# Merge gates of a two-layer hybrid trunk: seven block products for each pair of feature tiles in place of eight

## The chip, the cores and the metric

One core of one Trainium2 chip runs the whole program. The metric is the device time of one execution in microseconds (us), as a median of several runs. The core has five engines that work from queues of their own: PE (TensorE, matmuls; its weight loads are shown apart as PEld), DVE (VectorE), ACT (ScalarE), POOL (GpSimd) and SP (SyncE, which here issues all DMAs). Each engine takes its instructions in the order in which they stand in its queue, and a semaphore holds one back until what it needs is there.

## The reference, cut to what matters

Two layers run over 640 tokens (128 of context, 512 of latents) and 1024 features. Each layer makes `h` from `x`, projects it for four mixers (A: RWKV recurrence, B: attention, C: gMLP, D: Fourier), and merges their outputs with gates that come from `h`:

```python
h = rms_norm(x, p['norm_g']) * (1.0 + scale) + shift
...
proj = jnp.einsum('nbtw,nwd->nbtd', jnp.stack([o_a, o_b, o_c, o_d]), p['w_branch'])
gates = jax.nn.sigmoid(h @ p['w_merge'] + p['b_merge']).reshape(B, T, N_BRANCH, D_MODEL)
merged = jnp.einsum('nbtd,btnd->btd', proj, gates)
x = x + gate * (merged @ p['w_out'])
```

`h @ w_merge` is a product of (640 x 1024) by (1024 x 4096) in each layer, four gates for each of the 1024 features. The change is about this product. The Fourier branch is the real part of a 2-D DFT over positions and the 128 channels of each of four groups.

## The kernel before, in words

Features stand on partitions and tokens on columns. A feature tile is 128 features by T = 640 tokens; the tokens are worked on in two halves of 320 columns (`HALVES`). All big products are made with split operands: an f32 matrix is stored as `hi` (rounded to fp32r) plus `lo` (the rest), and a product is three matmuls, hi·hi, hi·lo and lo·hi, summed in PSUM (lines 168, 169, 170 in `dense_half`). `split` (lines 144 and 145) makes the parts: ACT casts `hi`, then POOL, or DVE where the call says so, subtracts to get `lo`. Weights come from HBM as raw blocks of 128 x 512 (`wr`, 4 buffers) and are split into `wh` and `wl` (3 buffers each), so that the split of a block may run up to three blocks ahead of PE.

The order of the work is written as Python generators: a main generator and a side generator are stepped in turn (`mix`), the side at a rate given for the stage. A scheduler then moves instructions within each engine's queue by its own estimate of times, so that casts, loads and side work stand ahead of where they were written. The queues are then fixed.

The end of each layer is the merge. For each branch n, in the order 1, 2, 3, 0 (attention, gMLP, Fourier, recurrence), and each of 8 feature tiles m it makes a gate (`gate`: 8 blocks of 128 inputs x 3 matmuls x 2 halves = 48 matmuls of 320 columns, then a tanh on ACT, line 1140) and a branch product (`branch`: 4 x 3 x 2 = 24 matmuls, then on DVE line 1146, which multiplies by the gate, and line 1149, which adds to `mg`). Beside each of the four stages runs a side generator (`beside`): `gmlp` beside branch 1, `fourier` beside branch 2, `rec_out` (group norm and bonus of the recurrence's output) beside branch 3, and beside branch 0 the conditioning (`ada`) of the next layer; layer 0 also has two steps of `ada` after `rec_out`. The results of a side generator go to HBM (`odr`) and are read back by `load_o` for the next stage. After the last branch each tile of `mg` is split into `mh` and `ml` for the output product.

`rec_out` loads five rows (`rv`) for each of four channel groups, and for each group makes three sums over 64 channels with matmuls against a block of ones (`sums`, lines 1082 and 1083, into the small PSUM banks named m), with some 20 DVE operations on 128 x 640 around them (lines 1093 to 1116).

PSUM has 8 banks. In the recurrence and the merge 3 are for the big products (`dps`) and 5 for side work (m).

## Time and profile before

| | us |
|---|---|
| median of 3 runs (2328.18 to 2330.07) | 2329.81 |
| profiled execution | 2330.01 |
| its span, first to last instruction | 2328.1 |
| PE busy in the span | 2183.5 |
| DVE busy | 1449.2 |
| ACT busy | 1098.4 |
| POOL busy | 894.4 |

A busy time is the union of an engine's instructions. Matmuls are pipelined, so that one of 0.31 us starts 0.147 us after the one before it; a busy PE is therefore not always a PE at its peak, and the count of matmuls in a stretch times the distance between their starts says more. The merge of layer 0 lies at 714.7 to 1138 us and that of layer 1 at 1865 to 2258.6 us of the span. Rows of a stretch list its length, then for each engine the busy time and in brackets the number of instructions, the granted clock of PE as a share of its full speed, and what the DMA engines did.

### The profile page before, as it was taken

How to read it: one execution, taken by the hardware profiler on the slowest of the kernel's cores; microseconds unless marked ns; L12 is line 12 of the kernel's file. 1: busy time of each engine (PE TensorE's matmuls, PEld its weight loads, DVE VectorE, ACT ScalarE, POOL GpSimd, SP SyncE). 2: the span in 40 equal slices, each digit the busy share in tenths (PEclk: the TensorE clock that was granted, in tenths of full speed). 3: DMA queues.
4: the chain of work that ended last, by engine and by line, in shares of the span. 5: the costliest groups of instructions: out<-in, count | busy, mean ns of one | idle time of the engine just before them, and what ended most of it. 6: DMA issues, size and time to landing. Idle time of an engine off the chain costs nothing. (4 is left out here: it accounts for less than half of the span.)

```text
span 2328.1 us, 49632 instructions
## 1 busy us (share of the span) xinstructions
PE 2183.5 (94%) x19662; PEld 2013.7 (86%) x19662; DVE 1449.2 (62%) x2826; ACT 1098.4 (47%) x2387; POOL 894.4 (38%) x894
## 2 busy tenths in 40 slices
PE   6899998898999999899999999989999999998998
PEld 3788898787888999878998888978888899997997
DVE  4777757888884335822367787578889643367234
ACT  4566755444434334422355676544444343344332
POOL 2322224444433335523552212244444334355452
PEclk8999999999999999999999999999999999998999
DMA  7133336333215425565432323362332254264233
GB/s 262 51 108 95 93 98 194 101 100 100 85 56 177 143 80 179 155 219 203 151 98 87 105 81 99 115 197 86 99 88 70 62 178 152 76 187 147 91 102 106
DMA packets 208009, 283.73 MB, mean 122 GB/s; under 512 B 26912, under 2 KB 119712, under 8 KB 207776
## 3 DMA queue, kind: packets, MB, share of 16 engines
q1 hardware_dynamic: 207776, 280.55, 38.1%
q8 instruction: 155, 2.54, 0.5%
q14 instruction: 78, 0.64, 0.1%
HBM read 224.75 MB, written 55.74 MB: 120 GB/s over the span
## 5 line engine op out<-in xcount | busy, mean ns | idle before, releaser
L145 POOL TENSOR_TENSOR wl<-wr,wh 128x512 fp32r<-128x512 f32 x371 | 523.0, 1413 | 975.0 <-ACT wh L144 853.4
L168 PE MATMUL dps<-hhi,wh 128*128 128x320 f32 x2368 | 772.6, 326 | 10.8 <-DVE f L1146 4.2
L169 PE MATMUL dps<-hlo,wh 128*128 128x320 f32 x2368 | 744.7, 314 | 7.9 <-POOL hlo L302 4.5
L170 PE MATMUL dps<-hhi,wl 128*128 128x320 f32 x2368 | 742.2, 313 | 0.0
L168 PEld LDWEIGHTS dps<-hhi,wh 128*128 128x128 f32 x2368 | 452.7, 191 | 25.6 <-ACT hhi L300 4.8
L169 PEld LDWEIGHTS dps<-hlo,wh 128*128 128x128 f32 x2368 | 453.3, 191 | 14.6 <-POOL hlo L302 7.1
L170 PEld LDWEIGHTS dps<-hhi,wl 128*128 128x128 f32 x2368 | 452.1, 191 | 0.5
L144 ACT CAST wh<-wr 128x512 fp32r<-128x512 f32 x372 | 229.6, 620 | 311.0 <-PE dps L169 200.2
L168 PE MATMUL dps<-ohi,wh 128*128 128x320 f32 x512 | 161.6, 316 | 2.1 <-ACT wh L144 1.9
L170 PE MATMUL dps<-ohi,wl 128*128 128x320 f32 x512 | 158.7, 311 | 1.0 <-POOL wl L145 1.0
L822 DVE TENSOR_TENSOR XZ<-XZ,m 128x512 f16<-128x512 f16 x200 | 129.5, 677 | 47.4 <-PE m L819 47.3
L169 PE MATMUL dps<-olo,wh 128*128 128x320 f32 x512 | 159.0, 311 | 0.0
L1146 DVE SCALAR_TENSOR_TENSOR f<-f,dps 128x320 f32<-128x320 f32 x96 | 46.3, 486 | 169.3 <-PE dps L170 169.3
L769 POOL TENSOR_TENSOR GG<-GG,con 64x256 f32<-64x256 f32 x80 | 60.8, 760 | 163.8 <-DVE GG L764 160.6
L1140 ACT ACTIVATE f<-dps,der 128x320 f32<-128x320 f32 x128 | 67.2, 525 | 111.4 <-PE dps L170 104.1
L168 PEld LDWEIGHTS dps<-ohi,wh 128*128 128x128 f32 x512 | 97.0, 189 | 10.6 <-issue 5.9
L170 PEld LDWEIGHTS dps<-ohi,wl 128*128 128x128 f32 x512 | 96.6, 189 | 2.4 <-POOL wl L145 1.5
L169 PEld LDWEIGHTS dps<-olo,wh 128*128 128x128 f32 x512 | 96.9, 189 | 1.7 <-issue 1.7
L812 DVE TENSOR_TENSOR T<-m,con 128x256 f16<-128x256 f32 x200 | 80.7, 416 | 18.6 <-PE m L811 18.0
L774 ACT CAST A<-GG 64x256 f16<-64x256 f32 x80 | 32.3, 403 | 90.4 <-POOL GG L769 90.3
L615 DVE TENSOR_TENSOR pl<-m,ph 128x512 fp32r<-128x512 f32 (+1 forms) x96 | 59.1, 620 | 24.8 <-ACT ph L614 23.5
L818 PE MATMUL m<-T,XZ 128*128 128x64 f16 x800 | 66.0, 195 | 5.2 <-DVE T L812 5.2
(493 smaller groups left out, 4624.4 us busy)
## 6 DMA issues: line engine op xcount, KB each, us to landing
wr<-in_w_in SPq DMA_DIRECT2D x180, 256.0 KB, 2.9
wr<-in_w_merge SPq DMA_DIRECT2D x128, 256.0 KB, 2.7
ar<-in_w_ada SPq DMA_DIRECT2D x48, 512.0 KB, 6.3
wr<-in_w_branch SPq DMA_DIRECT2D x64, 256.0 KB, 2.8
zdr<-f SPq DMA_DIRECT2D x48, 320.0 KB, 3.4
rk<-spill SPq DMA_DIRECT2D x20, 768.0 KB, 5.9
thdr<-t SPq DMA_DIRECT2D x32, 320.0 KB, 3.2
odr<-t SPq DMA_DIRECT2D x32, 320.0 KB, 3.5
```

The source lines that it names most:

```text
L144: S_.copy(hi, src)
L145: (leng or G).tensor_sub(lo, src, hi.bitcast(F32))
L168: mm(ps, hi[:, c], ahi(k)[:, q], start=(k == 0), stop=False)
L169: mm(ps, hi[:, c], alo(k)[:, q], start=False, stop=False)
L170: mm(ps, lo[:, c], ahi(k)[:, q], start=False, stop=(k == K - 1))
L615: V.tensor_sub(pl[:, 0:w], tp[:, 0:w], ph[:, 0:w].bitcast(F32))
L769: G.tensor_sub(GK[HALF[j], j], GK[HALF[j], j], bc(i64[HALF[j]], 4))
L812: V.tensor_mul(T1.rearrange("p u (j k o i) -> p (u j) k o i", j=2, o=2, i=b)[:, :, :, 0, :], ps[:, 0:256].rearrange("p (x k i) -> p x k i" ...
L818: mm(ps[:, 64 * u:64 * u + 64], X1[:, u, :], cols(T1[:, u, :], 0), start=True, stop=True)
L822: V.tensor_add(new, new, ps.rearrange("p (x n i) -> p x n i", x=2, i=b))
L1140: yield from dense(A["w_merge"][l, m, n], 8, H, lambda q, ps: S_.activation(gt[:, q], ps, AF.Tanh, scale=0.5, bias=bias))
L1146: yield from dense(A["w_branch"][l, n, m], 4, (lambda k: o[k][0], lambda k: o[k][1]), lambda q, ps: V.scalar_tensor_tensor(to[:, q], gt[:, ...
```

## The change

The gates of two neighbouring feature tiles m and m+1 are one product of a 256 x 1024 weight matrix by the 1024 x 640 `h`. Cut in 2 x 2 blocks on every side (two tiles, two halves of the inputs, two halves of the tokens) it takes eight block products of 4 x 3 = 12 matmuls each. The changed kernel makes it with seven, by Strassen's algorithm in Winograd's form. For that:

- `sums_of_h` makes three combinations T1, T2, T4 of the four blocks of `h` once in each layer, and `last_sum_of_h` a fourth, T3, which is written over a block of `h` that is needed no more.
- for each pair, DVE makes four combinations of the raw weight blocks (`s1`, `a21`, `a11`, `a12` in place); these are then split and multiplied by `product`.
- the products are collected in three PSUM banks: `al` takes four of the seven products one after the other and is read in between, `ga` takes two and is read in between, `be` takes one. Copies on ACT and additions on DVE put the parts of the four results together in `g`.
- the `al` bank is a pool of its own ("a"), so that the side work has 4 small banks where it had 5.
- the first two pairs of the first stage (`PLAIN = 2`) are made as before, in eight products, so 14 of the 16 pairs of a layer use seven.

The side work is put in another order: branches go 1, 0, 2, 3; beside branch 1 stand `sums_of_h` and `rec_out`, beside branch 0 `gmlp` (in layer 0 with two steps of `ada` behind it), beside branch 2 `fourier`, beside branch 3 the `ada` of the next layer. The rates are new. The buffers of `rec_out` are cut: three of its five rows have one buffer in place of two. `load_o` has 8 buffers where it had 12, and its loads for a branch are all issued after the second product of the branch's first pair. The Fourier mixing runs for two groups at a time, with the transform of its first column made for each two groups (15 small matmuls more in each layer). `gmlp` writes its gate input back to HBM and loads it again. The split of `mg` reuses the buffers of `mg`.

```diff
-RATE_M = (0.3, 0.55, 0.8, 0.5)
+RATE_M = (0.75, 0.45, 0.6, 0.45)
+PLAIN = 2
+SRB = 4
...
         def rec_out(y):
...
-                    rv = gp.tile([128, 5, T], F32, tag="rv", name="rv")
+                    rv = []
                     for i, (src, row) in enumerate(((spill, c), (spill, 12 + c), (spill, 4 + c), (thdr, 4 + c), (thdr, 12 + c))):
-                        nc.sync.dma_start(rv[:, i, :].rearrange("p (c t) -> p c t", t=128), src[l][:, :, row, :].rearrange("c p t -> p c t"))
+                        rv.append(gp.tile([128, T], F32, tag=f"rv{i}", name=f"rv{i}", bufs=2 if i > 2 else 1))
+                        nc.sync.dma_start(rv[i].rearrange("p (c t) -> p c t", t=128), src[l][:, :, row, :].rearrange("c p t -> p c t"))
...
+        def hsum(kk, top, q):
+            ks = slice(4 * top + 2 * kk, 4 * top + 2 * kk + 2)
+            t = tmp().rearrange("p (k t) -> p k t", k=2)
+            V.tensor_add(t, h_hi[:, ks, q].bitcast(F32), h_lo[:, ks, q].bitcast(F32))
+            return t
+        def sums_of_h(tp, B):
+            for n in ("1", "2", "4"):
+                B["T" + n] = tuple(tp.tile([128, 4, 320], F32R, name=f"T{n}{x}") for x in "hl")
+            for kk in range(2):
...
+                t1 = hsum(kk, 0, Q0)
+                t = hsum(kk, 0, Q1)
+                V.tensor_sub(t1, t, t1)
+                put("T1", t1)
+                yield
+                t2 = hsum(kk, 1, Q1)
+                V.tensor_sub(t2, t2, t1)
+                put("T2", t2)
...
+        def last_sum_of_h(B):
+            for kk in range(2):
+                ks = slice(2 * kk, 2 * kk + 2)
+                a, b = hsum(kk, 1, Q1), hsum(kk, 0, Q1)
+                V.tensor_sub(a, a, b)
+                S_.copy(h_hi[:, ks, Q1], a)
+                V.tensor_sub(h_lo[:, ks, Q1], a, h_hi[:, ks, Q1].bitcast(F32))
...
+        def product(ps, raw, b, leng, first=True):
+            hi, lo = (wp.tile([128, 512], F32R, tag="w" + x, name="w" + x, bufs=3) for x in "hl")
+            split(hi, lo, raw, leng)
+            for k in range(4):
+                c = slice(128 * k, 128 * k + 128)
+                mm(ps, hi[:, c], b[0][:, k, :], start=first and k == 0, stop=False, skip_group_check=True)
+                mm(ps, hi[:, c], b[1][:, k, :], start=False, stop=False, skip_group_check=True)
+                mm(ps, lo[:, c], b[0][:, k, :], start=False, stop=(k == 3), skip_group_check=True)
...
+                a11, a12 = raw_load(src[0], 512), raw_load(src[1], 512)
+                a21, a22, s1 = (m1.tile([128, 512], F32, tag="sr", name="sr", bufs=SRB) for _ in range(3))
...
+                yield from product(al, a11, B["11"], G)
+                S_.copy(g[0][:, Q0], al)
+                V.tensor_add(s1, a21, a22)
+                V.tensor_sub(a21, a11, a21)
+                V.tensor_sub(a11, s1, a11)
+                yield from product(be, a12, B["21"], V)
+                V.tensor_add(g[0][:, Q0], g[0][:, Q0], be)
+                tanh(0, Q0)
+                V.tensor_sub(a12, a12, a11)
+                start(n)
+                yield from product(ga, s1, B["T1"], G)
+                S_.copy(g[1][:, Q1], ga)
+                yield from product(al, a11, B["T2"], V, False)
+                S_.copy(g[0][:, Q1], al)
+                yield from product(ga, a12, B["22"], G, False)
+                V.tensor_add(g[0][:, Q1], g[0][:, Q1], ga)
+                tanh(0, Q1)
+                yield from product(al, a21, B["T3"], V, False)
+                V.tensor_add(g[1][:, Q1], g[1][:, Q1], al)
+                tanh(1, Q1)
+                b0 = branch(n, m, g[0])
+                yield from steps(b0, 3)
+                yield from product(al, a22, B["T4"], G, False)
+                tanh(1, Q0, al)
+                yield from b0
+                yield from branch(n, m + 1, g[1])
...
+        psum_l.close()
+        psum_l.enter_context(banks(3, 4, na=1))
...
-        beside = {1: (gmlp, RATE_M[0]), 2: (fourier, RATE_M[1]),
-                  3: (lambda: seq(rec_out(y), ada(l, (4, 5), 6) if l == 0 else iter(())), RATE_M[2]),
-                  0: (lambda: ada(l + 1, range(6), 6) if l + 1 < L else iter(()), RATE_M[3])}
+        beside = {1: (lambda: seq(sums_of_h(tp, B), rec_out(y)), RATE_M[0]),
+                  0: (lambda: seq(gmlp(), ada(l, (4, 5), 6) if l == 0 else iter(())), RATE_M[1]),
+                  2: (fourier, RATE_M[2]),
+                  3: (lambda: ada(l + 1, range(6), 3) if l + 1 < L else iter(()), RATE_M[3])}
...
-        mix(merge(m1, mg, (1, 2, 3, 0), before, lambda m: split(now["mh"][:, m, :], now["ml"][:, m, :], mg[:, m, :], V)),
-            aside(), lambda _: now["rate"])
+        mix(merge(m1, B, mg, (1, 0, 2, 3), before, done, PLAIN), aside(), lambda _: now["rate"])
```

In the pieces of the queues that follow, line numbers are those of the kernel they are taken from, and they shift: lines 144 and 145 (cast, subtraction) become 146 and 147, 1140 becomes 1231, 1146 becomes 1218, and those of `rec_out` move by 12. Names without a number are tiles as in the code; `aps` is the bank `al`, `sr` a block of `s1`, `a21` or `a22`, `wr` one of `a11`, `a12` or a raw block of a branch.

ACT in the last stage of layer 1, before: one feature tile and a half.

```order
L144 CAST wh<-wr 128x512
L144 CAST mh<-mg 128x640
L1140 ACTIVATE f<-dps,der 128x320
L144 CAST wh<-wr 128x512 x2
L1140 ACTIVATE f<-dps,der 128x320
L144 CAST wh<-wr 128x512
L144 CAST mh<-mg 128x640
```

The same place in the changed kernel, one pair of tiles:

```order
L146 CAST mh<-mg 128x640
L146 CAST wh<-sr 128x512
L146 CAST mh<-mg 128x640
L1256 COPY f<-aps 128x320
L146 CAST wh<-wr 128x512 x2
L1231 ACTIVATE f<-f,der 128x320
L146 CAST wh<-sr 128x512
L1266 COPY g<-dps 128x320
L146 CAST wh<-wr 128x512
L1268 COPY f<-aps 128x320
L146 CAST wh<-sr 128x512
L1231 ACTIVATE f<-f,der 128x320
```

Three copies out of PSUM (lines 1256, 1266, 1268) now stand between the casts, and the tanh reads what DVE has added.

DVE beside `rec_out` in layer 1, before: the end of one channel group with the two halves of a branch product (line 1146).

```order
L191 TENSOR_TENSOR t<-t 128x640
L192 SCALAR_TENSOR_TENSOR t<-t,rv 128x640
L193 SCALAR_TENSOR_TENSOR t<-t 128x640
L1111 TENSOR_TENSOR t<-t 128x640
L1112 TENSOR_SCALAR t<-t,vec 128x640
L1146 SCALAR_TENSOR_TENSOR f<-f,dps 128x320
L1113 TENSOR_TENSOR t<-t,rv 128x640
L1116 SCALAR_TENSOR_TENSOR t<-t 128x640
L1146 SCALAR_TENSOR_TENSOR f<-f,dps 128x320
```

DVE in layer 1 of the changed kernel, where the first pair made with seven products begins:

```order
L1113 SCALAR_TENSOR_TENSOR t<-m_26183,y 128x320
L1151 TENSOR_TENSOR t<-hhi,hlo 128x640 x3
L1185 TENSOR_TENSOR t<-t 128x640
L1151 TENSOR_TENSOR t<-hhi,hlo 128x640
L1114 TENSOR_TENSOR rv_25924<-rv_25924,m_26249 128x320
L1187 TENSOR_TENSOR hlo<-t,hhi 128x2x320
L1185 TENSOR_TENSOR t<-t 128x640
L1114 TENSOR_TENSOR rv_25924<-rv_25924,m_26253 128x320
L1261 TENSOR_TENSOR f<-f,dps 128x320
L1187 TENSOR_TENSOR hlo<-t,hhi 128x2x320
L1263 TENSOR_TENSOR wr<-wr 128x512
L147 TENSOR_TENSOR wl<-wr,wh 128x512
```

Eight operations of `last_sum_of_h` (lines 1151, 1185, 1187) stand among those of `rec_out` (1113, 1114) and ahead of the work for the pair (1261, 1263, 147).

PE beside `rec_out` in layer 1, before: one sum between a branch product and a gate.

```order
L170 MATMUL dps<-ohi,wl 128x320
L1082 MATMUL m_27886<-ch,blkr 128x320
L1083 MATMUL m_27886<-cl,blkr 128x320
L1082 MATMUL m_27890<-ch,blkr 128x320
L1083 MATMUL m_27890<-cl,blkr 128x320
L168 MATMUL dps<-hhi,wh 128x320
```

PE in the changed kernel, in the fourth product of that first pair:

```order
L1199 MATMUL aps<-T2h,wh 128x320
L1200 MATMUL aps<-T2l,wh 128x320
L1094 MATMUL m_26299<-ch,blkr 128x320
L1094 MATMUL m_26303<-ch,blkr 128x320
L1095 MATMUL m_26299<-cl,blkr 128x320
L1095 MATMUL m_26303<-cl,blkr 128x320
L1094 MATMUL m_26423<-ch,blkr 128x320
L1095 MATMUL m_26423<-cl,blkr 128x320
L1094 MATMUL m_26427<-ch,blkr 128x320
L1095 MATMUL m_26427<-cl,blkr 128x320
L1201 MATMUL aps<-T2h,wl 128x320
```

Two sums of `rec_out`, of two channel groups, now stand inside one product. On PE as a whole the changed kernel has 306 rows of matmuls fewer.

## Rows read from the trace of the kernel before

**Rows 1.** The page, engines over the whole span: busy us, share, instructions.

```profile
PE 2183.5 (94%) x19662; PEld 2013.7 (86%) x19662; DVE 1449.2 (62%) x2826; ACT 1098.4 (47%) x2387; POOL 894.4 (38%) x894
```

**Rows 2.** Busy time by stretch, layer 1's four merge stages; the sum over both layers'.

```profile
1865.00:1971.90 106.90, 103.67 (x760) 101.53 (x756) 44.91 (x73) 45.39 (x79) 41.27 (x29) 1.00 0.53 171
1971.90:2073.20 101.30, 101.30 (x721) 101.30 (x720) 43.30 (x99) 39.80 (x111) 43.36 (x29) 1.00 0.45 137
2073.20:2170.70 97.50, 87.04 (x549) 84.96 (x548) 66.22 (x86) 44.01 (x65) 50.79 (x34) 0.93 0.41 128
2170.70:2258.60 87.90, 87.90 (x601) 87.90 (x600) 24.17 (x36) 29.85 (x51) 39.63 (x27) 1.00 0.27 83
sum 816.90, PE 790.65 PEld 762.08 DVE 357.19 ACT 322.44 POOL 348.54; mean PE 98.83 PEld 95.26 DVE 44.65 ACT 40.31 POOL 43.57
```

**Rows 3.** PE in order of time, last stage: start us, duration us, instruction.

```profile
2201.11 0.31 PE L168 MATMUL dps<-hhi,wh 128*128 128x320 f32 x1
2201.26 0.31 PE L169 MATMUL dps<-hlo,wh 128*128 128x320 f32 x1
2201.40 0.31 PE L170 MATMUL dps<-hhi,wl 128*128 128x320 f32 x1
...
2203.60 0.31 PE L170 MATMUL dps<-hhi,wl 128*128 128x320 f32 x1
```

**Rows 4.** The page's groups: count, busy us, mean ns of one, idle before.

```profile
L145 POOL TENSOR_TENSOR wl<-wr,wh 128x512 fp32r<-128x512 f32 x371 | 523.0, 1413 | 975.0 <-ACT wh L144 853.4
L144 ACT CAST wh<-wr 128x512 fp32r<-128x512 f32 x372 | 229.6, 620 | 311.0 <-PE dps L169 200.2
L1140 ACT ACTIVATE f<-dps,der 128x320 f32<-128x320 f32 x128 | 67.2, 525 | 111.4 <-PE dps L170 104.1
```

**Rows 5.** Groups by shape on DVE and ACT, whole span.

```profile
L961 DVE TENSOR_TENSOR vt<-vt,gg 128x512 f32<-128x512 f32 x10 | 6.5, 682 | 0.1
L145 DVE TENSOR_TENSOR wl<-wr,wh 128x512 fp32r<-128x512 f32 x1 | 0.7, 690 | 0.0
L1102 DVE TENSOR_TENSOR rv<-rv,m 128x320 f32<-128x320 f32 x16 | 7.2, 479 | 4.3 <-PE m L1083 4.3
L351 ACT COPY f<-dps 128x320 f32<-128x320 f32 x48 | 20.2, 421 | 13.5 <-PE dps L170 13.3
```

**Rows 6.** Groups by shape on DVE, last stage of layer 1.

```profile
L1146 DVE SCALAR_TENSOR_TENSOR f<-f,dps 128x320 f32<-128x320 f32 x18 | 8.8, 488 | 53.1 <-PE dps L170 53.1
L1149 DVE TENSOR_TENSOR mg<-mg,f 128x640 f32<-128x640 f32 x10 | 8.2, 824 | 0.3
```

**Rows 7.** Busy time of `rec_out`'s stretch in layer 1, and two pieces of it.

```profile
2066.00:2154.00 88.00, 77.54 (x484) 75.46 (x483) 69.88 (x86) 41.48 (x61) 48.66 (x31) 0.92 0.43 136
...
2110.00:2120.00 10.00, 5.68 (x36) 4.96 (x34) 9.74 (x12) 0.88 (x2) 5.58 (x3) 1.00 0.30 102
...
2120.00:2130.00 10.00, 8.39 (x39) 8.05 (x40) 5.01 (x8) 5.82 (x9) 5.55 (x4) 0.66 0.87 272
```

**Rows 8.** Groups by shape on DVE, stretch of 2066 to 2154 us.

```profile
L1149 DVE TENSOR_TENSOR mg<-mg,f 128x640 f32<-128x640 f32 x6 | 9.0, 1493 | 0.1
...
L1146 DVE SCALAR_TENSOR_TENSOR f<-f,dps 128x320 f32<-128x320 f32 x12 | 5.6, 479 | 1.5 <-PE dps L170 1.5
...
L145 DVE TENSOR_TENSOR olo<-olo,ohi 128x640 fp32r<-128x640 f32 x2 | 2.1, 1050 | 0.5 <-ACT ohi L144 0.5
```

**Rows 9.** Waits in that stretch: who for whom, us in total, times, longest us.

```profile
PEld m L1082 <- ACT ch L144: 5.8, 2, 3.1
DVE rv L1093 <- DMA rv<-thdr: 5.6, 2, 3.6
PE m L1082 <- ACT ch L144: 5.3, 2, 2.8
```

More of the change, by code (lines that the diff above doesn't have):

```diff
@@ L1130, in load_o @@
                 to.append((a, b))
[L1132 to L1147 removed]
+        Q0, Q1 = HALVES
@@ new lines, in merge, with gates, branch @@
+        def merge(m1, B, mg, order, before, done, plain):
+            o = []
+            def gates(m):
+                return tmp(tag="f"), m1.tile([128, T], F32, tag="g", name="g", bufs=2)
+            def branch(n, m, gt):
+                first = n == order[0]
+                to = mg[m] if first else gt
+                w = [wload(A["w_branch"][l, n, m], 512)]
+                for q in HALVES:
+                    yield from dense_half(w, 4, (lambda k: o[k][0], lambda k: o[k][1]), lambda q, ps: V.scalar_tensor_tensor(
+                        to[:, q], gt[:, q], 1.0, ps, op0=ALU.add, op1=ALU.mult), q)
+                    yield
@@ L1302, in output @@
         V.tensor_scalar_mul(gh, lp[l]["mod"][:, 16:24, :], 0.5)
-        X = new_x(f"x{l + 1}")
+        X = new_x(f"x{l + 1}", under)
         xn = X["x"]
@@ L1365, in output, with new_x @@
         return X, h, in_weights(l + 1)
-    def new_x(name):
+    def new_x(name, under=None):
         pool = ExitStack()
+        if under is not None:
+            pool.push(under)
         xp = pool.enter_context(tc.tile_pool(name=name, bufs=1))
```

185 lines of the change are left out of this document (106 added, 79 removed).

## The prediction

> **What bounds the kernel now.** I read first the engines' totals: PE is busy 94% of the span, DVE 62%, ACT 47%, POOL 38% [rows 1]. The change lies in the merge, so I then read busy time by stretch, over the four stages of each layer's merge. The reader is to see two kinds of stage. In the last one of layer 1, which has no side work, PE is busy for all of 87.9 us at full clock, with 601 matmuls [rows 2]. In order of time they start 2.49 us apart over 17 steps (2201.11 to 2203.60), which is 0.1465 us each [rows 3], and 601 x 0.1465 = 88.0: PE issues without a hole and is the bound. The stage with `rec_out` is the other kind: in the 88.0 us from 2066 on PE issued 484 matmuls [rows 7], worth 484 x 0.1465 = 70.9 us, so 17.1 us are lost there, while DVE was busy 69.9 us. Two pieces of that stretch show how: from 2110 to 2120 DVE is busy 9.74 of 10 us and PE issues 36 matmuls where 68 would fit; in the next 10 us the granted clock is 0.66, which is a mix of its two levels, 1.2 and 2.4 GHz, after the hole [rows 7]. The waits name PE's own side matmuls (line 1082), which stand in its queue and wait for ACT's cast, 11.1 us over weight loads and matmuls, and DVE waiting 5.6 us for `rec_out`'s loads [rows 9]. So in most of the merge a matmul less is 0.1465 us less, and beside `rec_out` DVE and the order of the queues decide. Both layers' merges take 816.9 us [rows 2].
>
> **The change part by part.** The sum is made against the profiled execution, 2330.0 us (span 2328.1), which is 0.2 above the median of 2329.8.
>
> *Matmuls removed.* A pair of tiles needed 2 x 48 gate matmuls and needs 7 x 12 = 84; 12 less for each of 14 pairs in 2 layers is 336, at 0.1465 us: -49.2 us, if PE stays the bound.
>
> *Matmuls added.* The Fourier transform of the first column is made twice in a layer, 30 small matmuls in all (336 - 30 is the 306 that PE's queue loses). The trace does not show them at their new height of 34 rows; none has more columns than a 320-column one, so they cost 0 to 30 x 0.1465 = 4.4. I take 2.5.
>
> *Vector work added to a pair.* With its two branches a pair is now 132 matmuls or 19.3 us of PE (144 and 21.1 before). DVE does four combinations at 0.68, three subtractions for `lo` at 0.69 and three additions from PSUM at 0.48 [rows 5], four branch products at 0.49 and two additions to `mg` at 0.82 [rows 6]: 9.8 us. ACT does nine casts at 0.62, four tanh at 0.525 [rows 4] and three copies at 0.42 [rows 5]: 8.9. POOL subtracts six times at 1.41 [rows 4], as before: 8.5. All lie under PE's 19.3. What hides them is that the split runs up to three blocks ahead: a product lasts 12 x 0.1465 = 1.76 us, a cast with its subtraction 0.62 + 0.69 on DVE or 0.62 + 1.41 on POOL. Without that cover every product would wait 1.3 to 2.0 us, some 12 us a pair. The tight places are the products that go on in a bank just read: product 6 must wait for the copy of `al`, with one product, 1.76 us, between, and a cast of 0.62 stands ahead of the copy of 0.42 on ACT; product 7 waits for DVE's addition after product 6, with half a branch product between. That leaves some 0.7 us for semaphores and for whatever the side work put ahead, which on DVE is 0.8 to 1.5 us at a time [rows 6, 8]. Bounds: 0, as in the stage without side work, and 1.5 us a pair, one such operation in the way each time; over 28 pairs 0 to 42. I take 0.2 a pair, nearest to the first, since three of four stages have light side work: +5.6.
>
> *Memory and clashes.* Of DVE's additions the combinations read two operands from SBUF, as does the addition to `mg`, which takes 0.82 us in the last stage [rows 6] and 1.49 beside `rec_out` [rows 8], where POOL splits too. The Trainium skill, page "SBUF — State Buffer", section "Who interferes with whom", says that such a DVE instruction and a POOL instruction that reads SBUF shut each other out for a whole instruction; this trace agrees as far as the 0.82 against 1.49. The sum above uses the undisturbed durations; with a POOL subtraction of 1.41 ahead of one DVE operation for each of POOL's six in a pair, DVE's pair grows from 9.8 to 18.3 us, still under 19.3 where there is no side work, but over it with any. That is a rival below.
>
> *The first stage.* `rec_out` moves beside branch 1, where two pairs are plain. DVE's queue up to the end of `rec_out` in layer 1 (it reaches into the second pair with seven products) holds: `rec_out` itself, 69.9 - 9.0 - 5.6 - 2.1 = 53.2 [rows 7, 8] and some 3.5 of its first group that lies before that stretch; 12 branch products at 0.48, 5.8; eight combinations, six subtractions and five additions of two pairs, 5.4 + 4.1 + 2.4; the eight operations of `last_sum_of_h` at 0.82 to 1.49, 6.6 to 11.9; two of `sums_of_h` and two subtractions for the branch's operands, 3.7. That is 85 to 90 us. PE has 288 + 48 + 132 + 84 = 552 matmuls there, 80.9 us. Before it was 69.9 against 70.9, and 17.1 were lost. If the loss is the same it is 17; if it grows with the work (88.0 / 70.9 = 1.24 times the larger, 1.24 x 85 = 105) it is 24.5. The lower bound is DVE without a hole, a loss of 4 to 9; the upper is the same ratio on 90 us, 112, a loss of 31. I take 21, between the first two, which both rest on the stretch nearest to it: 4 more a layer, +8. The mechanism is the one of before: PE's queue has the sums of two channel groups inside the fourth product of the first pair, and stands still there until DVE, with the eight operations of `last_sum_of_h` ahead of it, has freed their banks; everything behind them waits too. Three of `rec_out`'s rows now have one buffer, so their loads wait for DVE in SP's queue, with weight blocks behind them; that is part of the same loss. The other six operations for T1, T2, T4 of each layer are moved up by the scheduler to the start of the recurrence, with POOL and ACT work; there they fill DVE by 12 x 0.82 = 9.8 us a layer. I take that as hidden (0 to 10 a layer if the recurrence's first chunks wait for it).
>
> *The other stages.* `gmlp` and `fourier` bring the same work as before, beside pairs of 19.3 us in place of 21.1. The loads of a branch's inputs are issued with 8 buffers after the last use of the old ones, four splits of 0.73 to 1.6 us within the six products (10.6 us) ahead of the first branch product; at six stage changes I take 0.5 us each, +3 (0 to 12).
>
> Sum: -49.2 + 2.5 + 5.6 + 8 + 3 = -30.1, which gives 2299.9 for the profiled execution, 2300 in round numbers.
>
> **The rivals.**
>
> *A. The side work costs no more than before.* The loss of the first stage stays at 17 or falls (plain pairs leave DVE 14 us at a time for `rec_out` without a branch product), and the pairs run without stalls. For it speaks the last stage, which has no hole; against it DVE's 85 us against 81. Then -49.2 + 2.5 = -46.7, 2283; with the loss at 9 in both layers 2267.
>
> *B. The first stage is bound by DVE outright.* At the upper loss of 31, 10 over what I take, and with 9.8 us a layer not hidden at the start of the recurrence it is 2 x 19.8 = 39.6 on the forecast, 2340; with half of it 2320. For it: DVE at 9.74 of 10 us already now [rows 7].
>
> *C. DVE and POOL shut each other out beside `gmlp` and `fourier`.* DVE has 43 to 45 us in those stages now, of which some 14 belong to the branches [rows 2, 6]; the rest, 30, is 7.5 us on each of four pairs. With 18.3 for the pair that makes 25.8. PE has in the Fourier stage 101.3 - 576 x 0.1465 = 16.9 us for side matmuls [rows 2], 4.2 a pair, and so 23.5: 2.3 us short on each of 16 pairs, +37, 2337; half of it, if every second operation meets one, 2318. The rule of the Trainium skill's page "SBUF — State Buffer" named above is this mechanism.
>
> *D. The shared bank decides: slower.* If at products 4 to 7 of each pair PE waits for the copy or the addition because ACT or DVE has another instruction ahead, at 0.62 us (one cast) each it is 2.5 us a pair, 28 x 2.5 = 70 in place of 5.6: 2364. It decides from 35.7 / 28 = 1.3 us a pair on: beyond that the kernel is slower than before. Against it: the queue of ACT has the copies right behind casts that wait for the same product's end, so that usually one cast is ahead, and 1.76 us lie between.
>
> **How the numbers follow.** The forecast (2290 to 2316 about 2300) has 0.45; A 0.27; B 0.13; C 0.06; D 0.09. A measurement of this kernel can tell about 0.2%, 4.7 us, from no change. Faster by more than that (under 2325): nearly all of the forecast, A, most of B and half of C, 0.83. Within it: the rest of B and C, 0.08. Slower: D, 0.09. The range from 2266 to 2328 leaves out the end of A, the upper ends of B and C, and D; the forecast's own part of it is 2290 to 2316.
>
> **What would show each step right or wrong.** The stages with seven products should show 132 matmuls in 19.3 to 20 us a pair; in the last stage of layer 1 four pairs should end 77 to 80 us after they begin, where it is 87.9 us for much the same now. If they take 85, the bank or the port is the cause, and the waits should name PE behind ACT's copy (lines 1256 to 1268) or DVE's addition (1261 to 1273). The stretch with `rec_out` should show DVE over 90% busy in several pieces, a granted clock under 1 behind holes, and 17 to 25 us lost in each layer; if it is 10 or less, A holds. The recurrence should take as long as before to within 5 us. The forecast is wrong in its mechanism if the last stage does not shrink, and in its size if the first stage's loss is outside 9 to 31.

## The result, and the profile after

The changed kernel takes 2369.11 us (median of four, 2363.45 to 2370.31) against 2328.99: a ratio of 1.0169, 95% interval 1.0150 to 1.0187. It is slower by 39 us by the ratio (40 by the medians); the forecast was 2300, and its range ended at 2328. Where a kernel below is set against another of a different batch, the difference is taken between their ratios to the kernel before and multiplied by 2329 us; each ratio is uncertain by some 0.002, so such a difference by some 7 us.

The page of the changed kernel, engines over the whole span, as in [rows 1]:

```profile
PE 2168.4 (92%) x19356; PEld 1979.3 (84%) x19356; DVE 1681.2 (71%) x3182; ACT 1195.0 (50%) x2607; POOL 911.2 (38%) x906
```

PE issues the 306 instructions less that were counted. DVE is busy 232 us more, with 356 instructions more. Busy time by stretch, the four merge stages of layer 1 in their new order (`rec_out`, `gmlp`, Fourier, none), and the sum over both layers, to be set against [rows 2] and, for the first, [rows 7]; the four stages of layer 0 stand in front:

```profile
721.80:846.40 124.60, 99.00 (x594) 93.95 (x593) 102.04 (x125) 66.15 (x100) 68.20 (x42) 0.90 0.52 158
846.40:953.40 107.00, 98.55 (x638) 90.69 (x637) 72.02 (x118) 46.60 (x87) 36.92 (x26) 0.95 0.55 186
953.40:1052.10 98.70, 96.28 (x680) 94.33 (x679) 59.65 (x145) 52.25 (x150) 37.03 (x26) 1.00 0.40 127
1052.10:1159.70 107.60, 104.39 (x674) 85.42 (x673) 46.91 (x78) 45.40 (x81) 39.19 (x27) 1.00 0.52 170
1896.20:2020.00 123.80, 99.29 (x594) 94.75 (x593) 101.07 (x125) 65.90 (x100) 67.64 (x42) 0.90 0.52 159
2020.00:2116.60 96.60, 88.61 (x590) 86.81 (x589) 73.91 (x115) 45.74 (x85) 38.06 (x26) 0.96 0.50 162
2116.60:2215.20 98.60, 96.06 (x680) 94.32 (x679) 59.84 (x145) 52.47 (x150) 36.93 (x26) 1.00 0.35 111
2215.20:2297.10 81.90, 79.55 (x530) 78.77 (x529) 46.99 (x68) 41.21 (x75) 37.80 (x27) 0.98 0.30 88
sum 838.80, PE 761.73 PEld 719.04 DVE 562.44 ACT 415.71 POOL 361.78; mean PE 95.22 PEld 89.88 DVE 70.30 ACT 51.96 POOL 45.22
```

The merges take 838.8 us where they took 816.9, though PE has less to do. The two sums do not begin at the same mark: in each layer [rows 2] begins 5.4 us ahead of the end of DVE's last addition to `y`, the recurrence's output, and the sum here right behind it. From that mark to the last branch matmul the two merges take 839 us where they took 804, so that some 35 of the 39 us lie in them. The recurrence itself takes as long as before, within 1 us.

The first stage is the odd one: 594 matmuls at 0.1465 us are 87.0, so 36.8 of its 123.8 us are lost, with DVE busy for 101. By this measure and from the same marks, layer 0 and layer 1 lose beside `rec_out` 37.6 and 36.8 us (before: 21.3 and 17.0), beside `gmlp`, in layer 0 now with two steps of `ada`, 13.5 and 10.2 (before: 1.0 and 2.0), and in the last stage 8.9 and 4.3 (before: nothing). The Fourier stage loses nothing in either kernel. So the first stage is the largest place of the loss and not the only one.

The last stage of layer 1 was to take 77 to 80 us, or 85 if the shared bank decided. It takes 81.9; 2.35 of its 4.3 lost us are one wait at the change of stage, shown further below. The same view over two pairs of seven products in the last stage:

```profile
2242.30:2261.80 19.50, 19.50 (x134) 19.39 (x134) 12.17 (x18) 9.77 (x20) 7.98 (x6) 1.00 0.29 84
2261.80:2281.20 19.40, 19.40 (x133) 19.27 (x132) 12.29 (x18) 9.70 (x19) 7.95 (x6) 1.00 0.22 64
```

With nothing beside them, pairs run at 19.5 and 19.4 us for 132 matmuls (19.3 at 0.1465), PE without a hole, so there the chain of products through the shared bank holds. DVE needs 12.2 us for a pair and not 9.8: its additions are longer than in [rows 6], as its groups in the last stage show:

```profile
L1222 DVE TENSOR_TENSOR mg<-mg,f 128x640 f32<-128x640 f32 x4 | 4.4, 1098 | 0.0
L1222 DVE TENSOR_TENSOR mg<-mg,g 128x640 f32<-128x640 f32 x3 | 4.2, 1405 | 0.1
```

Where the first stage loses its time, two places show. First GpSimd at the stage's head, in order of time (start, duration, instruction):

```profile
1899.74 2.16 POOL L1164 TENSOR_TENSOR T4l<-t,T4h 128x640 fp32r<-128x640 f32 x1
1901.86 2.16 POOL L1164 TENSOR_TENSOR T1l<-t,T1h 128x640 fp32r<-128x640 f32 x1
1903.98 1.54 POOL L1164 TENSOR_TENSOR T2l<-t,T2h 128x640 fp32r<-128x640 f32 x1
1905.49 1.52 POOL L147 TENSOR_TENSOR olo<-olo,ohi 128x640 fp32r<-128x640 f32 x1
1906.98 2.11 POOL L1164 TENSOR_TENSOR T4l<-t,T4h 128x640 fp32r<-128x640 f32 x1
1909.05 1.31 POOL L147 TENSOR_TENSOR wl<-wr,wh 128x512 fp32r<-128x512 f32 x1
```

and PE in the same time:

```profile
1904.17 0.31 PE L171 MATMUL dps<-hlo,wh 128*128 128x320 f32 x1
1910.41 0.63 PE L172 MATMUL dps<-hhi,wl 128*128 128x320 f32 x1 [5.93 <-POOL wl L147]
```

The low parts of T1, T2 and T4 (line 1164) stand ahead of a weight's low part, and PE waits 5.93 us for that. Then DVE, in two pieces around the first pair of seven products:

```profile
1955.00:1965.00 10.00, 8.16 (x55) 7.64 (x53) 10.00 (x16) 3.12 (x6) 3.18 (x2) 1.00 0.42 117
1965.00:1975.00 10.00, 5.48 (x18) 4.40 (x18) 10.00 (x13) 4.73 (x7) 3.81 (x2) 0.67 0.12 41
```

and in order of time there:

```profile
1963.89 4.49 DVE L1151 TENSOR_TENSOR t<-hhi,hlo 128x640 f32<-128x640 f32 x3
```

DVE has no hole for 20 us; in the second half PE issues 18 matmuls where 68 would fit, and the clock granted then is 0.67, a mix of its two levels (1.2 and 2.4 GHz). PE's holes there are those that the prediction named: it stands at a sum of `rec_out` until DVE frees the bank (line 1114), then at a weight's low part in DVE's queue.

```profile
1970.40 0.39 PE L1094 MATMUL m<-ch,blkr 128*128 128x320 f32 x1 [1.61 <-DVE rv L1114]
1975.55 0.64 PE L1201 MATMUL aps<-T2h,wl 128*128 128x320 f32 x1 [1.52 <-DVE wl L147]
```

This is the picture of [rows 7] between 2110 and 2130, worse.

### The profile page after: what moved, and what is told of

It is laid out like the page before. It is cut to its first block, busy times and chain, and to the rows that moved or that the text cites. A ratio compares the mean times of both kernels' runs of the same rounds, so it can differ in the third digit from the quotient of the medians.

```text
span 2368.4 us, 49971 instructions
## 1 busy us (share of the span) xinstructions
PE 2168.4 (92%) x19356; PEld 1979.3 (84%) x19356; DVE 1681.2 (71%) x3182; ACT 1195.0 (50%) x2607; POOL 911.2 (38%) x906
## 5 line engine op out<-in xcount | busy, mean ns | idle before, releaser
L147 POOL TENSOR_TENSOR wl<-wr,wh 128x512 fp32r<-128x512 f32 x315 | 435.0, 1382 | 874.1 <-ACT wh L146 740.1
L170 PE MATMUL dps<-hhi,wh 128*128 128x320 f32 x1472 | 489.8, 333 | 7.2 <-ACT hhi L302 4.2
L172 PE MATMUL dps<-hhi,wl 128*128 128x320 f32 x1472 | 466.3, 317 | 13.5 <-POOL wl L147 13.5
L171 PE MATMUL dps<-hlo,wh 128*128 128x320 f32 x1472 | 468.1, 318 | 9.5 <-DVE hlo L304 4.7
L170 PEld LDWEIGHTS dps<-hhi,wh 128*128 128x128 f32 x1472 | 283.3, 192 | 16.6 <-ACT hhi L302 5.0
L171 PEld LDWEIGHTS dps<-hlo,wh 128*128 128x128 f32 x1472 | 283.4, 193 | 16.1 <-POOL hlo L304 7.6
L172 PEld LDWEIGHTS dps<-hhi,wl 128*128 128x128 f32 x1472 | 283.1, 192 | 15.3 <-POOL wl L147 15.0
L147 POOL TENSOR_TENSOR wl<-sr,wh 128x512 fp32r<-128x512 f32 x56 | 84.6, 1510 | 144.2 <-ACT wh L146 127.8
L146 ACT CAST wh<-sr 128x512 fp32r<-128x512 f32 x84 | 52.0, 620 | 87.2 <-PE dps L171 48.7
L1199 PE MATMUL dps<-hhi,wh 128*128 128x320 f32 x224 | 73.6, 329 | 7.0 <-ACT g L1266 6.3
L1201 PE MATMUL dps<-hhi,wl 128*128 128x320 f32 x224 | 72.0, 321 | 3.0 <-POOL wl L147 2.6
```

What stands on the lines that cost most here:

```text
L146: S_.copy(hi, src)
L147: (leng or G).tensor_sub(lo, src, hi.bitcast(F32))
L170: mm(ps, hi[:, c], ahi(k)[:, q], start=(k == 0), stop=False)
L171: mm(ps, hi[:, c], alo(k)[:, q], start=False, stop=False)
L172: mm(ps, lo[:, c], ahi(k)[:, q], start=False, stop=(k == K - 1))
L1199: mm(ps, hi[:, c], b[0][:, k, :], start=first and k == 0, stop=False, skip_group_check=True)
```

## The experiments

### Which part of the change costs it

The first four each leave out one part: seven products with their sums, the sums of h, seven products in the first stage, and `rec_out`.

```diff
-PLAIN = 2
+PLAIN = 16          # e1, and sums_of_h(tp, B) out of the first stage
+PLAIN = 4           # e3
-                    last_sum_of_h(B)                          # e2: T1 to T4 are
+                    B["T1"] = B["T3"] = h_hi[:, 0:4, Q1], ... # plain blocks of h
-                  seq(sums_of_h(tp, B), rec_out(y))
+                  seq(sums_of_h(tp, B), raw_out(y))           # e4: y sent out as it is
```

> All 16 pairs of a layer are made with eight products (PLAIN = 16) and the sums of h are not made; the new order of the side work, the smaller buffers and the four small banks stay. Theory 1 (the vector work of the seven products, in one queue with rec_out, costs the time): the loss beside rec_out falls to what it was before, 17 us a layer, and the whole is near the kernel before, 2330 to 2350. Theory 2 (the new order and the smaller buffers cost it, whatever the products): the loss stays and 49 us of matmuls come back, 2385 to 2415. Theory 3 (the products stall in their shared bank): everything that was lost comes back, 2325 to 2335.

> The 14 pairs use seven products, but the combinations T1 to T4 of h are not computed: plain blocks of h stand in their places (this part of the computation is left out, the matmuls are the same in number and shape). Theory 1: without the sums' POOL and DVE operations the first stage loses some 15 us less in each layer, 2335 to 2345. Theory 2: 2360 to 2370. Theory 3: 2360 to 2370.

> PLAIN = 4: all four pairs of the first stage, the one beside rec_out, use eight products; 12 pairs of a layer use seven. 48 matmuls come back, +7 us. Theory 1: the vector work of the seven products no longer meets rec_out, the loss there falls by 10 to 20 us a layer, 2336 to 2356. Theory 2: 2374 to 2378. Theory 3: four of 28 pairs less with the fault, 2365 to 2372.

> rec_out is left out (the recurrence's output goes unnormed and without bonus to its branch); all else as in the changed kernel. Theory 1: the first stage's loss of some 42 us a layer nearly goes, with 7 us of side matmuls: 2270 to 2295. Theory 2: the order of the other stages still costs, 2290 to 2310. Theory 3: the first stage keeps its stalls, 2330 to 2350.

Measured: e1 2356.26, ratio 1.0129 (1.0100 to 1.0159); e2 2337.98, 1.0056 (1.0033 to 1.0079); e3 2353.52, 1.0117 (1.0088 to 1.0147); e4 2295.73, 0.9869 (0.9840 to 0.9898). e2 and e3 came out within Theory 1's ranges, e4 just above its range and inside Theory 2's, and e1 between Theories 1 and 2, 6 us above the first. So a part of the loss, some 30 us, is there with eight products (e1): it belongs to what else was changed, that is order, rates, buffers, banks and side work. The sums of h cost 1.0169 - 1.0056, 26 us. With `rec_out` gone (e4) the changed kernel takes 30 us less than the kernel before with its `rec_out`. That does not show that seven products pay there, since the kernel before was not run without it: by an estimate from the lines here, `rec_out` costs that kernel 21.3 and 17.0 us of lost time and 48 matmuls, 7.0 us, in each layer, 52 us in all. Theory 3, a stall in the shared bank, is small: in the whole changed kernel PE waits 10 us for a copy and an addition that stand between products (in the lines: us in total, times, longest).

```profile
PE dps L1199 <- ACT g L1266: 6.3, 5, 2.4
PE aps L1199 <- DVE g L1273: 3.8, 5, 1.3
```

### Are the holes in the first stage the price, or DVE's work?

e5 spreads the six steps of the sums of h between `rec_out`'s; e6 casts the branch inputs later; e8 does both, with a plain first stage, the last sum beside branch products and a lower rate beside `gmlp`.

```diff
-        beside = {1: (lambda: seq(sums_of_h(tp, B), rec_out(y)), RATE_M[0])   # e5, e8
+        def with_sums():
+            rec, sm = rec_out(y), sums_of_h(tp, B)
+            yield from steps(rec, 6)
+            for _ in range(6):
+                yield next(sm)
+                yield from steps(rec, 4)     # e8: 8
...
-                split(a, b, of, V if c % 2 else G)      # e6, e8: in load_o no more,
+                splits()                                # but after the fourth product
```

> The changed kernel with the six steps of the sums of h no longer at the head of the first merge stage but one at a time between steps of the recurrence's output (six steps of it first, four between). Theory A (the first stage loses through the burst of sums at its head: the gap of 6.24 us at 1904.17 in front of a weight's low part, then 3.1 us, then a lower clock): the first stage falls from 124 us to about 115 in each layer, and the time from 2369 to about 2352. Theory B (the same vector work in the same stage costs the same wherever it stands, since VectorE and GpSimd slow each other): the time stays within 5 us of 2369.

> The changed kernel with the branch input's loads where they are, but their splits issued after the fourth of the seven products in place of the second. Theory A (at a change of stage ScalarE's copy of a gate's sum waits behind the cast of a branch input that has not landed, and TensorE waits for the copy, 1.0 to 2.7 us at each change): those gaps go, and the time falls by 5 to 9 us. Theory B (the gaps are only moved to the branch product that reads the split): the time stays within 2 us.

> The changed kernel with its first merge stage made of eight products throughout, the sums of h spread between the steps of the recurrence's output (six first, eight between), the last sum of h beside the branch products in front of the second stage, the branch inputs' splits after the fourth product, and a rate of 0.36 in place of 0.45 beside the second stage. If the losses of the first stage, of the stage changes and of the gating unit are the waits named in the trace, it takes 2320 to 2335 us (2353.5 with a first stage of eight products alone, less 2 x 8 for the sums, less 5 to 9 for the splits, less some us for the rate). If vector work costs the same wherever it stands, it stays at 2345 to 2355 us.

Measured: e5 2376.29, 1.0222 (1.0199 to 1.0244); e6 2368.75, 1.0182 (1.0163 to 1.0201); e8 2356.78, 1.0132 (1.0108 to 1.0155). My theory of single waits falls in all three. That the work costs the same wherever it stands came out in e6 and nearly in e8 (1.8 us above its range); e5 is slower than either theory had it, by 12 us by the ratios. In e5 the hole at the head has gone to other places (PE's longest waits in that stage are 5.4, 4.7 and 3.7 us), and the stage became longer, 133.4 us. In e6 the copy no longer waits at the last change of stage, where the changed kernel shows

```profile
2224.81 0.64 PE L1199 MATMUL dps<-hhi,wh 128*128 128x320 f32 x1 [2.35 <-ACT g L1266]
```

but a weight's low part is late instead:

```profile
2225.53 0.42 PE L1200 MATMUL dps<-hhi,wl 128*128 128x320 f32 x1 [1.34 <-POOL wl L147]
```

and e8 is no better than its plain first stage alone (e3).

### Which engine's work: the sums of h taken apart

```diff
-                    G.tensor_sub(lo, t, hi.bitcast(F32))   # e9: low parts read from a block of h
-                t1 = hsum(kk, 0, Q0) ... V.tensor_sub(t4, t4, t2)
+                put(n, a block of h)                       # e10: no VectorE work for T1, T2, T4
-                S_.copy(h_hi[:, ks, Q1], a) ...            # e11: the last sum's eight operations
```

> The changed kernel without GpSimd's six subtractions for each layer's sums of h (the low parts of T1, T2 and T4 are read from a block of h instead); VectorE's additions and ScalarE's copies stay, and the matmuls are the same in number. Leaving out all of the sums gained 31 us (2338 against 2369). Theory A (the price is GpSimd's: its subtractions stand ahead of the weights' low parts, and VectorE slows beside them): 2342 to 2352, most of the 31 us. Theory B (the price is VectorE's own additions and the eight instructions of the last sum): 2360 or more.

> The changed kernel with T1, T2 and T4 made from single blocks of h, so that VectorE's additions and subtractions for them are left out and ScalarE's copies and GpSimd's subtractions stay. Theory A (the price is GpSimd's): 2360 or more. Theory B (the price is VectorE's additions): 2345 to 2355.

> The changed kernel without the last sum of h alone (eight instructions of VectorE and ScalarE in front of the first pair of seven products; T3 is read from plain h). Theory A (GpSimd's burst at the head is the price): 2364 or more. Theory C (the price is the last sum, in front of which the weight's split and the recurrence's output wait at 1964 to 1975 us): 2350 to 2358.

Measured: e9 2360.64, 1.0134 (1.0111 to 1.0156); e10 2361.64, 1.0145 (1.0123 to 1.0168); e11 2354.73, 1.0119 (1.0094 to 1.0144). e9 lies where Theory B had it, e10 where Theory A did, e11 where Theory C did. Against 1.0169 these are 8, 6 and 12 us, each uncertain by some 7, so that the 6 by itself is not clear of noise. Together they are 26, which is what leaving out all of it gained; that agreement holds to some 12 us. No one engine has the price; Theories A and B had each named one. The first stage of layer 1, one line of busy time by stretch from each kernel (DVE's time is the third pair of figures):

e1, eight products throughout:

```profile
1887.00:1994.40 107.40, 97.64 (x618) 95.69 (x617) 62.46 (x90) 53.90 (x79) 53.26 (x37) 0.94 0.62 190
```

e2, no sums of h:

```profile
1876.20:1986.00 109.80, 95.23 (x595) 92.30 (x594) 82.14 (x112) 59.17 (x91) 55.32 (x36) 0.94 0.60 187
```

e9, no GpSimd in the sums:

```profile
1891.20:2012.40 121.20, 100.92 (x595) 95.95 (x594) 93.53 (x125) 66.13 (x100) 56.77 (x36) 0.89 0.53 163
```

e10, no VectorE work for T1, T2 and T4:

```profile
1890.30:2013.50 123.20, 100.14 (x594) 96.05 (x593) 98.34 (x123) 65.82 (x100) 67.80 (x42) 0.89 0.53 160
```

e11, no last sum:

```profile
1886.30:2003.80 117.50, 95.76 (x594) 90.92 (x594) 93.60 (x116) 63.95 (x98) 67.08 (x42) 0.94 0.54 168
```

e5, sums spread:

```profile
1896.70:2030.10 133.40, 104.23 (x594) 97.71 (x594) 115.13 (x136) 65.51 (x100) 69.14 (x42) 0.86 0.48 148
```

Length less matmuls at 0.1465 us gives a loss of 16.9, 22.6, 34.0, 36.2, 30.5 and 46.4 us, where DVE is busy 62, 82, 94, 98, 94 and 115; the changed kernel has 36.8 at 101. From the first to the last 29.5 us more are lost for 52.7 us more of DVE: about half a us of PE goes with each us that DVE is busy there, while DVE is busy 58 to 86% of the stage. That is how the two go together in seven kernels; busy time holds waiting too, and e9 shows it: its first stage has the same 125 DVE instructions as the changed kernel's, and without GpSimd's six subtractions they take 93.5 us in place of 101.1.

### What costs 30 us with eight products

e7 is the kernel before with three buffers for the modulation weights; e12 is the kernel before with the changed kernel's `gmlp`, `fourier` and `rec_out`.

```diff
-                  0: (lambda: ada(l + 1, range(6), 6) if l + 1 < L else iter(()), RATE_M[3])}
+                  0: (lambda: ada(l + 1, range(6), 3) if l + 1 < L else iter(()), RATE_M[3])}   # e7
```

> The kernel before, with three buffers in place of six for the modulation weights beside the last merge stage, and nothing else changed. Theory A (the changed kernel's loss in layer 0's last stage, 25.1 us against 13.2 before, comes from the three buffers): 8 to 12 us slower than the kernel before, all in layer 0's last stage. Theory B (it comes from the order of stages and from the transfers of weights that this stage now shares): within 3 us of the kernel before.

> The kernel before, with its eight products, its order and its rates, and only the gating unit, the Fourier mixing per pair and the recurrence output's smaller buffers taken from the changed kernel. If the side work as rewritten costs nothing but the 30 more small matmuls in each layer: 2 to 5 us slower than before. If smaller buffers cost (one set of buffers for three of the recurrence output's five inputs, the gate's input sent out and read again): 8 to 20 us slower, and the stage in which it falls says which.

Measured: e7 2334.61, 1.0042 (1.0028 to 1.0055), 10 us; e12 2338.50, 1.0040 (1.0026 to 1.0055), 9 us. The last stage of layer 0 by stretch, in the kernel before

```profile
1041.00:1137.00 96.00, 96.00 (x667) 84.77 (x667) 23.63 (x42) 30.06 (x52) 34.94 (x23) 1.00 0.49 168
```

and in e7:

```profile
1041.20:1145.60 104.40, 103.08 (x666) 85.35 (x665) 23.50 (x41) 30.18 (x51) 34.82 (x23) 1.00 0.48 164
```

Same matmuls, 8.4 us longer, with DMA as busy as before: this fits fewer transfers under way and not a fuller DMA. Theory A holds. How the 8.4 us arise is not shown: PE's waits that the profile names for these weights are 1.3 us. The first three stages of layer 0 in the kernel before

```profile
720.10:819.70 99.60, 97.20 (x673) 96.16 (x672) 42.18 (x68) 43.70 (x74) 40.06 (x28) 1.00 0.53 173
819.70:919.70 100.00, 100.00 (x713) 100.00 (x712) 42.58 (x97) 39.59 (x111) 41.58 (x28) 1.00 0.44 136
919.70:1040.90 121.20, 111.03 (x682) 99.91 (x680) 67.09 (x93) 47.98 (x72) 55.30 (x36) 0.94 0.51 171
```

and in e12:

```profile
720.00:817.20 97.20, 96.97 (x673) 96.19 (x673) 42.91 (x68) 40.41 (x71) 39.08 (x28) 1.00 0.54 170
817.20:923.20 106.00, 103.93 (x728) 102.89 (x727) 42.67 (x111) 41.64 (x128) 40.25 (x27) 0.98 0.43 134
923.20:1051.10 127.90, 113.14 (x685) 100.74 (x683) 68.92 (x93) 49.49 (x74) 56.94 (x37) 0.93 0.49 162
```

In layer 0 the price lies in the Fourier stage, of which 15 more small matmuls (15 in each layer, not the 30 that the expectation says) are at most 15 x 0.1465 = 2.2 of 6.0, and in `rec_out`'s, 6.7; `gmlp` is 2.4 shorter. In layer 1 the four stages are only 1.0 us longer than before (388.2 against 387.2). The 9 us are in the range expected of smaller buffers, but e12 does not part the buffers from the rest of the rewriting. Of the 30 us of e1, the 10 of the three buffers are so found. Of e12's 9 only a part carries over, since beside `rec_out` e1 loses less than the kernel before, 16.8 us in layer 0 against 21.3. At least 11 stay unassigned; by place, e1 loses 10.3 and 4.3 us beside `gmlp`, where the kernel before loses 1.0 and 2.0.

### Why seven products without the sums of h gain so little

From e1 to e2 49 us of matmuls gained 17.

```diff
-                V.tensor_add(s1, a21, a22)             # e13: e2 without these four
-                V.tensor_sub(a21, a11, a21)
-                V.tensor_sub(a11, s1, a11)
-                V.tensor_sub(a12, a12, a11)
-                S_.copy(g[0][:, Q0], al) ...           # e14: e2 without the copies and
-                V.tensor_add(g[0][:, Q0], g[0][:, Q0], be) ...   # additions between products
-PLAIN = 2
+PLAIN = 8                                              # e15, the sums of h beside gmlp
```

> The kernel without the sums of h (2338), and in it without VectorE's four sums of weight blocks in each of the 28 pairs (the third product takes a plain block, the others their blocks as loaded). Against the kernel with eight products and no sums (2356) that one saves 49 us of matmuls and gains 18. Theory D (the 31 us lost are VectorE's: the weight sums stand in its queue ahead of the splits of the weights and of the side work): 2318 to 2326. Theory E (the loss lies in the chain of the products' results, copies and additions between the products that share a bank): 2334 or more.

> The kernel without the sums of h (2338), and in it without the three copies and three additions that make a pair's gates from its seven products (each tanh reads one product's bank; the weight sums stay). Theory D: 2332 or more. Theory E: 2316 to 2326.

> The changed kernel with eight products in the first two merge stages (beside the recurrence's output and the gating unit) and seven in the last two; the six steps of the sums of h go one at a time between the gating unit's steps, the last sum at the head of the third stage. All products of eight and no sums took 2356; 16 pairs of seven save 28.1 us of matmuls. Theory F (the sums and the pairs cost only where VectorE is full, in the first stage): 2328 to 2340. Theory G (they cost the same beside any side work): 2345 to 2356.

Measured: e13 2319.13, 0.9965 (0.9953 to 0.9978); e14 2343.54, 1.0074 (1.0059 to 1.0089), no gain over e2's 1.0056; e15 2344.01, 1.0082 (1.0063 to 1.0101). The weight sums cost 21 us, the copies and additions between products nothing measurable: Theory D. The stages of layer 1 in e2

```profile
1876.20:1986.00 109.80, 95.23 (x595) 92.30 (x594) 82.14 (x112) 59.17 (x91) 55.32 (x36) 0.94 0.60 187
1986.00:2087.00 101.00, 91.64 (x590) 89.26 (x589) 75.72 (x118) 45.75 (x85) 39.16 (x26) 0.93 0.45 148
2087.00:2185.40 98.40, 95.94 (x680) 94.30 (x679) 59.58 (x145) 52.52 (x150) 37.32 (x26) 1.00 0.34 112
2185.40:2267.80 82.40, 78.58 (x530) 77.41 (x529) 46.74 (x69) 41.16 (x75) 37.76 (x27) 1.00 0.28 88
```

and in e13:

```profile
1866.90:1973.40 106.50, 93.59 (x594) 90.90 (x593) 70.63 (x103) 59.03 (x91) 55.01 (x36) 0.95 0.63 193
1973.40:2068.80 95.40, 88.67 (x590) 87.12 (x589) 60.18 (x100) 45.36 (x85) 37.04 (x26) 0.96 0.50 159
2068.80:2164.70 95.90, 95.12 (x680) 94.16 (x679) 50.19 (x128) 52.16 (x150) 36.41 (x26) 1.00 0.36 114
2164.70:2245.10 80.40, 77.84 (x530) 77.47 (x529) 35.59 (x55) 41.91 (x75) 38.90 (x27) 1.00 0.28 87
```

All four shrink, by 3.3, 5.6, 2.5 and 2.0 us, at the same matmuls and with DVE at 57 to 75% of the stage in e2, so not full in any stage as a whole. e15 fell between its two theories: moving sums and pairs away from `rec_out` makes them cheaper, not free.

Part of this price can be a wait, not work. In the changed kernel the third weight sum (line 1259) writes over a block that GpSimd still reads for the first product, and DVE's queue stands behind it. DVE's waits in that kernel (us in total, times, longest):

```profile
DVE wr L1259 <- POOL wl L147: 56.8, 21, 3.8
```

e16 lets DVE subtract the first product's low part itself; e17 gives the sum a block of its own.

```diff
-                yield from product(al, a11, B["11"], G)
+                yield from product(al, a11, B["11"], V)   # e16
-                V.tensor_sub(a11, s1, a11)
+                V.tensor_sub(s2, s1, a11)                 # e17
```

> The changed kernel with the first product's low part subtracted on VectorE in place of GpSimd. In the changed kernel the third weight sum writes over the block that GpSimd still reads for the first product, and VectorE stands idle in front of it 56.8 us, 21 times of 28, until GpSimd is done. Theory H (the 20 us that the weight sums cost are this wait, with the splits and the side work queued behind it): those waits go and the time falls from 2369 by 10 to 20 us, to 2349 to 2359, though VectorE has 28 x 0.69 = 19 us more work. Theory I (the price is VectorE's work as such): 2366 to 2380, since the work grows.

> The changed kernel with the third weight sum written to a block of its own in place of over the first block of the pair (four of the ring's blocks a pair in place of three, the ring still of four, so that the next pair's blocks are loaded later). Theory H (VectorE's wait for GpSimd is the price): 2349 to 2362, less what the later loads cost. Theory I (the work as such): 2364 to 2376.

Measured: e16 2358.39, 1.0140 (1.0120 to 1.0161); e17 2375.10, 1.0199 (1.0178 to 1.0221). In e16 the wait is gone, and the time falls by 7 us by the ratios (10 by the medians) although DVE has 19 us more to do: Theory H, at the edge of its range by the median and short of it by the ratio; the two intervals just overlap, so the size is not sure. Another wait grows in its place: DVE waits 66.6 us for ACT's casts of weights (line 147) in e16, where it waited 34.8. e17 came out in Theory I's range, but it tells nothing apart: 20.6 us of the wait are left there, and DVE waits 10.4 us for blocks loaded later, where it waited 0.8.

No version of the changed kernel here beats the kernel before with the whole computation in it; the best is e15.

## Why the forecast was wrong

The forecast's arithmetic on PE held: 336 matmuls went, pairs run at 0.1465 us a matmul, and the shared bank (rival D, which alone gave 2364) costs little: the 10 us of waits above, and leaving out the copies and additions gained nothing (e14); that the time came out near D's is chance. What failed is the list of what the gain is paid with. One reading was wrong without harm to the sum: the 11.1 us of side-matmul waits are the same two holes counted twice, for the weight loads and for the matmuls, and PE stood 5.3 us in them.

- *"The first stage ... +8."* The sums of h cost 26 us, 12 of them the last sum's (e11), and the loss in layer 1 is 36.8, outside the 9 to 31 that the prediction set. Up to the end of `rec_out`, where the prediction counted 85 to 90 us for DVE, DVE is busy 98.3:

```profile
1896.20:2014.00 117.80, 93.29 (x553) 88.75 (x552) 98.29 (x120) 61.69 (x94) 66.34 (x41) 0.90 0.51 153
```

The ratio of [rows 7], 88.0 / 70.9 = 1.24, gives 122 us for these 98.3, where 117.8 were measured; it is a rough guide (for e5 it gives 143 for 133.4), but by it the loss would have been 41 us, where the prediction took 21 and 36.8 were measured. The queue was undercounted, with durations of undisturbed instructions, and the result taken between two ratios, not from the one that grows with the work.

- *"The other six operations ... I take that as hidden."* Most of VectorE's work did move ahead of the recurrence, but ACT's casts and GpSimd's subtractions stand at the head of the merge (from 1895.9 us in layer 1). GpSimd's, which the sum priced nowhere, cost 8 of the 26 us (e9); VectorE's part, taken as covered, costs 6, not clear of noise (e10).
- *"Vector work added to a pair ... All lie under PE's 19.3 ... +5.6."* The four weight sums alone cost 21 us (e13). DVE was not full in any stage as a whole, but it is one queue in program order: a sum in it stands ahead of weight splits, one of the sums waits for GpSimd, and GpSimd lengthens others (below). How the 21 us divide among these no run shows. A budget per pair shows only that the work fits, not that it is free. 0 to 42 were the bounds, and the value next to the stage without side work was the wrong one: three of four stages have side work.
- *"`gmlp` and `fourier` bring the same work as before"*, and only 2.5 for the Fourier matmuls. Beside `gmlp` the changed kernel loses 13.5 and 10.2 us, where the kernel before loses 1.0 and 2.0; the sum had nothing for that. In the kernel before, the rewritten side work costs 9 (e12), and the three buffers for the modulation weights, which the sum left out, 10 (e7).
- *"At six stage changes ... +3."* PE's waits for the copy of line 1266 are 6.3 us in five places, more than the 3, but moving the casts gained nothing (e6), so this term is not settled.

Together, if the parts add and all of e12's 9 is taken: -49.2 + 26 + 21 + 10 + 9 = 17 of the 39 us by which it is slower. Some 22 us, uncertain by about 12 since they are a rest of measured differences, are not assigned to a cause; e1 has 11 of them. By place, the stage beside `gmlp` still loses 9.0 us in layer 1 of e13, which makes neither kind of sum; its new place, its rate, the load buffers and the fewer banks were not tried one by one. Rival B had the mechanism, DVE in the first stage, and its upper price of 2340 was too low. Rival C's mechanism, DVE and GpSimd in each other's way, shows in the longer additions and in e9's shorter DVE time, but its share of the 39 us was not measured by itself. The rule of the Trainium skill, page "SBUF — State Buffer", section "Who interferes with whom", that both shut each other out, agrees with this case's trace for the sums on DVE, as below.

## What to carry to other kernels

Price vector work that is added to a matmul loop at a rate, not at nothing because it fits: here, waits included, a us of it went with 0.2 us (21 us for the 99 us that the four sums take in e2) to 0.5 us (beside heavy side work) of the matmul engine. Count what the change takes away to make room: a pool cut from six to three buffers is a term of its own. And look for an instruction that writes over an operand which another engine still reads: it stops its whole queue, here for 56.8 us in all.

## What the hardware showed that was not expected

One shape on DVE has two durations. The weight sum of line 1258 in the changed kernel, min/median/max in ns:

```profile
L1258 DVE TENSOR_TENSOR sr<-wr,sr x28: 669/692/1767, 760.5 to 2266.4; 128x512 f32<-128x512 f32 x28
```

Ten of the 28 took over 1 us, so that an undisturbed duration is a lower bound only. The trace shows what lengthens it, for example here:

```profile
2266.12 1.41 POOL L147 TENSOR_TENSOR wl<-wr,wh 128x512 fp32r<-128x512 f32 x1 [1.53 <-ACT wh L146]
2266.42 1.65 DVE L1258 TENSOR_TENSOR sr<-wr,sr 128x512 f32<-128x512 f32 x1
```

The sum begins while GpSimd's subtraction runs, and ends 0.55 us after it. So it is with all 15 of the 112 weight sums that took over 1 us: each began during a GpSimd instruction and ended 0.55 us after its end; the other 97 took at most 0.87. Line 1218, which reads one of its operands from PSUM, took 0.47 to 0.49 us in all 128 cases, with GpSimd at work or not. A sum on DVE that reads two blocks of SBUF is thus to be priced with the rest of whatever GpSimd instruction is already running. And removals added up, as far as the noise allows: three parts of one cost, on different engines, gave 8, 6 and 12 us singly, each uncertain by some 7, and 26 together.
